# Weights laid out by the host in the units in which they are loaded

## The chip, the cores and the metric

The kernel runs on one core of one Trainium2 chip. The metric is the device time of one execution, in microseconds. Three runs of the kernel before took 2642.75, 2643.20 and 2644.79 us; the median is 2643.2 us.

## The reference

One sequence of 256 tokens with 1024 features passes through two blocks, each of two layers. All arrays are fp32. Cut to what carries the weights:

```python
# first block, l = 0, 1: a Fourier/convolution mixer (l = 0) or windowed attention (l = 1), then experts
shift, scale, gate = adaln(cond, ada_w[l, s], ada_b[l, s])       # ada_w[l, s]: [1024, 3072]
def ec_moe(h, router_w, router_b, w_gate, w_up, w_down):          # 16 experts, 32 tokens each
    ...
    xg = h[bidx, idx]
    hid = jax.nn.silu(jnp.einsum("becd,edf->becf", xg, w_gate)) * jnp.einsum("becd,edf->becf", xg, w_up)
    y = jnp.einsum("becf,efd->becd", hid, w_down) * gate[..., None].astype(h.dtype)
    return jnp.zeros_like(h).at[bidx, idx].add(y)

# second block, l = 0, 1: swiglu_ffn, three attentions side by side, swiglu_ffn
def swiglu_ffn(x, g, wi, wo):                                     # wi: [1024, 5632], wo: [2816, 1024]
    a, b = jnp.split(rms_norm_2(x, g) @ wi, 2, axis=-1)
    return (jax.nn.silu(a) * b) @ wo
```

Each expert's `w_gate`, `w_up` and `w_down` is a matrix of 1024 by 1024, which makes 12.6 MB for an expert and 201 MB for the experts of a layer. All other weights of both blocks together are some 290 MB, most of them in the second block.

## The kernel before

**Units of weight.** Every large weight reaches SBUF in units of 1 or 2 MB, each a tile `w` of 128 partitions. A unit is a block of rows and columns of the weight as it stands in HBM. Row k * 128 + p of the block goes to partition p, so what one partition receives is several rows, each contiguous in HBM for the width of the block alone: 512 columns (2 KB) for `ada_w`, `fc_w_in`, `attn_w_qkv` and most of the second block, 256 columns (1 KB) for the second block's output matrices, 1024 columns (4 KB) for the experts, `fc_w_out` and `attn_w_out`. `load_unit` (lines 209 to 212) issues the DMA on SP's queue. In `moe` (lines 798 to 808) a unit holds 256 rows of `w_gate` and the same 256 rows of `w_up` of one expert, and two DMAs of 1 MB fill it (line 801); the 16 matmuls of line 808 that use the unit read both parts at once, so they wait for both. A unit of `w_down` is one DMA of 2 MB (line 841), but for the last unit of the last expert, which comes in four DMAs of 0.5 MB. `attn_w_out` (lines 387 to 392) comes in four DMAs of 1 MB, each to 64 partitions, since the rows of two heads have to be interleaved.

**Buffers and queue.** In the first block a ring of seven 2 MB buffers (line 868) holds the units, and `moe` has two more of its own (`unit`, lines 789 to 794). SP issues the loads in one order for the whole program; a load is issued when its buffer has been read by the last matmul of the unit that held it before. So the loads run ahead of TensorE by up to nine units, and stop when all buffers are full. The second block has a ring of four buffers (line 1740).

**Order.** The instructions are recorded in program order and a scheduler sets the order on each engine, from its own estimate of when each operand is there. A load's estimated time is part of that.

**Other queues at the start.** `setup` (lines 244 to 267) issues the constants `cst` and `vec` on SP ahead of the first units, `x`, `positions` (256 integers to 128 partitions) and `msk` on ScalarE's queue, and small tables and `fou` on GpSimd's queue. `positions` starts the rotary tables (`rope_setup`, line 517 on), whose `Sin` on ScalarE (line 536) stands ahead of the first norm there. VectorE's line 531 and GpSimd's line 424 are two steps of that time that the prediction names.

**The names in the trace.** `wh` and `wl` are the two parts into which ScalarE (line 218) and VectorE (line 219) split a weight for all products but those of the experts and of adaLN. Line 278 is adaLN's product, line 808 the experts' first product, line 846 the second. Lines 1113 to 1115 are the three passes of a product of the second block. In the trace's names of DMA queues, q1 is SP's, q10 ScalarE's, q0 GpSimd's; q8 and q14 fetch the engines' instructions and tables, not data of the kernel.

Of the kernel before, what the change touches and what calls it, by code (L numbers as in the profile page):

```python
# [28 lines left out]
# columns of the fp32 constant block  # L29
# [15 lines left out]
# exp(-ln(10000) * i * 2 / d) in float32, as bit patterns  # L45
# [7 lines left out]
def host_constants2():  # L53
# [23 lines left out]
    # block n of group g: the first half of tokens 16 n.., the second half of tokens 16 (n + 1).., and the offsets  # L77
# [5 lines left out]
def host_constants():  # L83
# [12 lines left out]
    # Fourier matrices over the sequence (256) and over a group's features (128)  # L96
# [6 lines left out]
    # additive masks: identity and triangles, as bfloat16 words  # L103
# [5 lines left out]

class Halves:  # L110
    """Chunks 0-3 and 4-7 in two tiles."""
# [7 lines left out]
class Norm:  # L119
    """A norm whose row factors (rs, RS) may come after the products that they scale have begun."""  # L120


class Net:
# [32 lines left out]
    def rsqrt(self, out, ss, scale, eps, pool, tag, bufs=2):  # L156
        """out = (ss * scale + eps) ** -0.5 by Newton's iteration on VectorE."""
# [38 lines left out]
    def row_ss(self, pool):  # L196
        """Sums of squares of all rows: column t for token tile t."""
# [24 lines left out]
    def dense(self, xh, xl, wdram, n0, n, evac, cpool):  # L222
        """Token-layout product [256, n] of the split x^T and columns n0.. of a [1024, N] weight."""
# [4 lines left out]
    def dense_steps(self, xh, xl, wdram, n0, n, evac, cpool):  # L228
        nc = self.nc
        w = self.load_unit(wdram[:, n0:n0 + n].rearrange("(k p) n -> p k n", p=P), [P, KC, n])  # L230
# [50 lines left out]
    def ada_affine(self, l, s, g, router=False):  # L281
        """Per-feature factor and offset (as columns) of the modulated norm."""
# [18 lines left out]
        # the router takes the factor into its weights and the offset into its bias  # L301
# [15 lines left out]
    def ada_gate(self, l, s):  # L317
        """The gate row on all partitions; for the experts columns 256 j.. on partitions 32 j.."""
# [3 lines left out]
        for j0 in range(2):  # L322
            # the bias joins on the diagonal
# [18 lines left out]
    def normed(self, pool, dst):  # L342
        """dst = x / rms(x), token layout."""
# [11 lines left out]
    def transposed(self, xn, emit):  # L355
        """Transposes the 1024 features of both token tiles; emit(k, psum [128, 256])."""
# [10 lines left out]
    def mod_split(self, pool, xn, A, B, tag):  # L367
        """(xn * A + B)^T in split form."""
# [43 lines left out]
    def mixer(self, ada):  # L412
        nc, a = self.nc, self.a
        with ExitStack() as es:
# [20 lines left out]
            win = a["fc_w_in"][0]  # L435
# [5 lines left out]
            # depthwise convolution: four taps of 32 channels fill the contraction, four groups run side by side  # L441
# [1378 lines left out]
```

## Time and profile before

| | |
|---|---|
| time, median of three runs | 2643.2 us |
| span of the profiled execution, first to last instruction | 2640.8 us |
| TensorE matmul busy | 2193.6 us (83%) |
| HBM read | 695.28 MB, 264 GB/s over the span |
| packets on SP's queue | 270800, 693.52 MB, 71.7% of 16 DMA engines |
| issues of `moe_w_gate` and `moe_w_up` | 128 each, 1024 KB |
| issues of `moe_w_down` | 62 of 2048 KB, 8 of 512 KB |

The span is cut into stages by what runs: the mixer to about 190 us, the experts of layer 0 to about 642 us, windowed attention to about 803 us, the experts of layer 1 to about 1254 us, and from there the second block. A view by slices or by stretches gives for each the busy time of the engines, the TensorE clock that was granted, the busy share of the 16 DMA engines and the rate in GB/s. A view of the DMA packets in a window gives their number by queue, the bytes, and the time that the packets took as a share of 16 engines; a share above 100% means that packets overlap a little on an engine. Packets under 512 bytes are the 4-byte writes that end each transfer, but for a few small constants.

### The profile page before, as it was taken

Reading aid. Unit: us, or ns where it says so; the run is one execution under the profiler, and the core shown is the slowest. Engines: PE = TensorE matmul, PEld = TensorE weight load, DVE = VectorE, ACT = ScalarE, POOL = GpSimd, SP = SyncE. Lnnn points to the kernel's source line nnn. Section 1 sums busy time; section 2 is a strip of 40 time slices with the busy share of each in tenths; the row PEclk is TensorE's granted clock in tenths of the full one; section 3 lists DMA queues with packets and bytes.
Section 4 is the critical chain, followed back from the end, with each engine's and each line's share of the span. In section 5 each row is a group of like instructions: output and inputs, shape, how many; then the busy total and the mean of one; then the engine's idle time right before and its main releaser. Section 6 shows DMA issues by size and latency. Waiting matters only on the chain.

```text
span 2640.8 us, 39018 instructions
## 1 busy us (share of the span) xinstructions
PE 2193.6 (83%) x16264; PEld 1610.6 (61%) x16264; DVE 1175.8 (45%) x2258; ACT 885.5 (34%) x1494; POOL 92.4 (3%) x137
## 2 busy tenths in 40 slices
PE   5977655555987555555999999999999999999999
PEld 3542111112553111111899978799999997789997
DVE  4451101102662101010755567775565566677663
ACT  4430000002441000000544565554444446655443
POOL 1100000000000000000100010000000000000000
PEclk9988768888998888888999999999999999999999
DMA  9989999999968999999555553255555555324553
GB/s 361 333 341 409 409 409 409 409 409 401 307 247 356 409 409 409 409 409 408 192 185 181 162 173 99 78 178 177 180 187 189 174 178 181 109 84 138 182 186 118
DMA packets 272224, 698.86 MB, mean 265 GB/s; under 512 B 9792, under 2 KB 66896, under 8 KB 272048
## 3 DMA queue, kind: packets, MB, share of 16 engines
q1 hardware_dynamic: 270800, 693.52, 71.7%
q8 instruction: 128, 2.10, 0.3%
q0 software_dynamic: 544, 1.60, 0.3%
q10 hardware_dynamic: 704, 1.25, 0.1%
q14 instruction: 48, 0.39, 0.0%
HBM read 695.28 MB, written 1.05 MB: 264 GB/s over the span
## 4 chain that ended last, share of the span: by engine, by line
PE 48%; ACT 1%; DVE 1%; DMA 0%; issue 0%; POOL 0%; ACTq 0%; DVEq 0%
PE mm L1115 11%; PE mm L1114 11%; PE mm L1113 11%; PE at L1687 1%; PE at L1113 1%; PE at L1115 1%; PE at L1114 1%; PE mm L1070 1%; PE mm L1069 1%; PE mm L1071 1%; PE tr L1229 1%; PE oa L1699 1%; PE oa L1352 1%; ACT wh L218 1%; DVE wl L219 1%; PE at L1391 0%
## 5 line engine op out<-in xcount | busy, mean ns | idle before, releaser
L219 DVE TENSOR_TENSOR wl<-w,wh 128x1024 fp32r<-128x1024 f32 (+3 forms) x494 | 551.0, 1118 | 396.1 <-ACT wh L218 379.9
L218 ACT CAST wh<-w 128x1024 fp32r<-128x1024 f32 (+3 forms) x494 | 472.5, 959 | 590.0 <-PE mm L1114 415.8
L808 PE MATMUL mm<-w,xg 128*32 128x512 f32 x2048 | 326.4, 766 | 237.9 <-DMA w<-in_moe_w_up_dram 236.4
L1114 PE MATMUL mm<-hl,wh 128*128 128x256 f32 x1728 | 490.3, 284 | 2.5 <-DVE hl L958 2.5
L1115 PE MATMUL mm<-hh,wl 128*128 128x256 f32 x1728 | 490.6, 284 | 0.0
L1113 PE MATMUL mm<-hh,wh 128*128 128x256 f32 x1728 | 490.5, 284 | 0.0
L808 PEld LDWEIGHTS mm<-w,xg 128*32 128x32 f32 x2048 | 69.8, 128 | 459.5 <-issue 362.8
L1114 PEld LDWEIGHTS mm<-hl,wh 128*128 128x128 f32 x1728 | 326.1, 189 | 4.3 <-DVE hl L958 3.1
L1115 PEld LDWEIGHTS mm<-hh,wl 128*128 128x128 f32 x1728 | 326.1, 189 | 3.7 <-issue 3.4
L1113 PEld LDWEIGHTS mm<-hh,wh 128*128 128x128 f32 x1728 | 326.0, 189 | 0.6 <-issue 0.3
L828 ACT ACTIVATE sil<-mm 128x256 f32<-128x256 f32 x32 | 12.3, 384 | 802.9 <-PE mm L808 802.9
L846 PE MATMUL at<-w,hidT 128*32 128x256 f32 x2048 | 165.9, 481 | 93.5 <-DMA w<-in_moe_w_down_dram 84.0
L829 DVE TENSOR_TENSOR hid<-mm,sil 128x256 f32<-128x256 f32 x32 | 13.6, 425 | 506.5 <-ACT sil L828 506.5
L846 PEld LDWEIGHTS at<-w,hidT 128*32 128x32 f32 x2048 | 76.1, 135 | 174.6 <-DMA w<-in_moe_w_down_dram 81.5
L854 DVE TENSOR_TENSOR xh<-at,agm 32x256 f32<-32x256 f32 x128 | 53.8, 420 | 281.0 <-PE at L846 279.6
L1114 PE MATMUL mm<-gl,wh 128*128 128x256 f32 x528 | 149.3, 283 | 0.0
L1115 PE MATMUL mm<-gh,wl 128*128 128x256 f32 x528 | 148.8, 282 | 0.0
L1113 PE MATMUL mm<-gh,wh 128*128 128x256 f32 x528 | 148.5, 281 | 0.0
L1113 PEld LDWEIGHTS mm<-gh,wh 128*128 128x128 f32 x528 | 99.9, 189 | 0.0
L1115 PEld LDWEIGHTS mm<-gh,wl 128*128 128x128 f32 x528 | 99.5, 189 | 0.0
L1114 PEld LDWEIGHTS mm<-gl,wh 128*128 128x128 f32 x528 | 98.9, 187 | 0.0
L278 PE MATMUL oa<-w,condp 128*32 128x512 f32 x384 | 55.4, 637 | 7.0 <-DMA w<-in_ada_w_dram 6.2
(574 smaller groups left out, 3343.3 us busy)
## 6 DMA issues: line engine op xcount, KB each, us to landing
w<-in_moe_w_gate_dram SPq DMA_DIRECT2D x128, 1024.0 KB, 18.9
w<-in_moe_w_up_dram SPq DMA_DIRECT2D x128, 1024.0 KB, 18.6
w<-in_moe_w_down_dram SPq DMA_DIRECT2D x62, 2048.0 KB, 23.0
w<-in_ffn_wi_dram SPq DMA_DIRECT2D x88, 1024.0 KB, 5.2
w<-in_ada_w_dram SPq DMA_DIRECT2D x24, 2048.0 KB, 19.7
w<-in_w_in_dram SPq DMA_DIRECT2D x40, 1024.0 KB, 5.1
w<-in_ffn_wo_dram SPq DMA_DIRECT2D x35, 1024.0 KB, 5.1
w<-in_ffn_wo_dram SPq DMA_DIRECT2D x12, 768.0 KB, 4.9
```

The lines of the kernel that those rows point to most:

```text
L218: self.nc.scalar.copy(wh, w)
L219: self.nc.vector.tensor_sub(wl, w, wh.bitcast(F32))
L278: nc.tensor.matmul(ps[32 * j:32 * j + 32, :], self.condp[:, k, 3 - row:35 - row], w[:, k, :], start=first and r == 0, stop=last and r == 1)
L808: nc.tensor.matmul(ps[32 * j:32 * j + 32], xg[:, k, e * CAP:(e + 1) * CAP], w[:, :, kk, j * 256:(j + 1) * 256], start=k == 0, stop=k == KC ...
L846: nc.tensor.matmul(psd[32 * j:32 * j + 32, :], hT2[:, k % 2, 32 * (k // 2):32 * (k // 2) + 32], w[:, kk, j * 256:(j + 1) * 256], start=k = ...
L854: nc.vector.tensor_tensor(dst, psd[32 * j:32 * j + 32, :], gate[32 * j:32 * j + 32, :], op=ALU.mult)
L1069: nc.tensor.matmul(ps[t], xh[:, k, sl], wh[:, c, :], start=k == 0, stop=False)
L1070: nc.tensor.matmul(ps[t], xl[:, k, sl], wh[:, c, :], start=False, stop=False)
L1071: nc.tensor.matmul(ps[t], xh[:, k, sl], wl[:, c, :], start=False, stop=k == kc - 1)
L1113: nc.tensor.matmul(o, wh[:, cs], xh[:, k, :], start=k == 0 and j == 0, stop=False, skip_group_check=True)
L1114: nc.tensor.matmul(o, wh[:, cs], xl[:, k, :], start=False, stop=False, skip_group_check=True)
L1115: nc.tensor.matmul(o, wl[:, cs], xh[:, k, :], start=False, stop=k == kc - 1 and j == 1, skip_group_check=True)
```

## The change

The host packs each large weight into the units in which the kernel loads them, a partition's part of a unit contiguous. `pack` writes one array for a weight and layer: unit after unit, and in each unit partition after partition. `UNITS` lists the blocks, in the order and of the sizes in which the kernel asks for them, and `Packed.unit` finds one. A load is then a DMA of 128 rows, each as long as a partition's whole part: 16 KB for the 2 MB units of the first block, 8 KB for a 1 MB unit of the second. The bytes in SBUF are where they were. The gate and up rows of an expert's unit lie beside each other in `moe_w_gate_up` and come in one DMA of 2 MB. `attn_w_out` is packed with its heads already in the order in which the two halves were filled, and comes in two DMAs of 2 MB to 128 partitions. The last unit of `w_down` of the last expert still comes in four DMAs, each with 4 KB for a partition. Small tables, `x` and the constants are loaded as before. The diff also takes out comments and the unused `load8`; lines move by that, nothing else. Its core:

```diff
+def _blocks(kc, m, n0, n):
+    return [(k, min(m, kc - k), n0, n) for k in range(0, kc, m)]
+UNITS = {
+    "ada_w": lambda l: [(0, KC, 512 * j, 512) for j in range(6)],
+    "fc_w_in": lambda l: [(0, KC, 512 * j, 512) for j in range(3)],
+    "attn_w_out": lambda l: _blocks(KC, 4, 0, D),
+    "ffn1_wi_2": _ff_in,
...
+class Packed:
+    def __init__(self, ap, name, l):
+        self.ap, self.at, off = ap, {}, 0
+        for k0, m, n0, n in UNITS[name](l):
+            self.at[k0, n0] = (off, m, n)
+            off += P * m * n
+    def unit(self, k0, m, n0, n):
+        off, m_, n_ = self.at[k0, n0]
+        assert (m, n) == (m_, n_), (k0, m, n0, n)
+        return self.ap[off:off + P * m * n].rearrange("(p x) -> p x", p=P)
+def pack(w, name, l):
+    out = []
+    for k0, m, n0, n in UNITS[name](l):
+        out.append(w[P * k0:P * (k0 + m), n0:n0 + n].reshape(m, P, n).transpose(1, 0, 2).ravel())
+    return np.concatenate(out)
...
-    def load_unit(self, src, shape, eng=None):
+    def W(self, name, *i):
+        return Packed(self.a["_".join(map(str, (name, *i)))], name, i[-1])
+    def load_unit(self, src, shape):
         w = self.T(self.ring, shape, "w", self.wbufs)
-        (eng or self.nc.sync).dma_start(w, src)
+        self.nc.sync.dma_start(w if len(shape) == 2 else w.rearrange("p k n -> p (k n)"), src)
...
-        w = self.load_unit(self.a["ada_w"][l, s, :, j0 * 512:(j0 + 1) * 512].rearrange("(k p) n -> p k n", p=P),
-                           [P, KC, 512])
+        w = self.load_unit(self.W("ada_w", l, s).unit(0, KC, j0 * 512, 512), [P, KC, 512])
...
-            n = P // len(wdram[u])
-            for i, src in enumerate(wdram[u]):
-                nc.sync.dma_start(w[n * i:n * i + n], src)
+            nc.sync.dma_start(w.rearrange("p k n -> p (k n)"), wdram.unit(4 * u, 4, 0, D))
...
-                    for i, nme in enumerate(("moe_w_gate", "moe_w_up")):
-                        nc.sync.dma_start(w[:, i], a[nme][l, e, u * 256:(u + 1) * 256, :]
-                                          .rearrange("(k p) f -> p k f", p=P))
+                    nc.sync.dma_start(w.rearrange("p g k f -> p (g k f)"), a["moe_w_gate_up"][l, e, u])
...
-                        r0 = u * 512 + c * P
-                        nc.sync.dma_start(w[:, c:c + step], a["moe_w_down"][l, e, r0:r0 + step * P, :]
-                                          .rearrange("(k p) f -> p k f", p=P))
+                        nc.sync.dma_start(w[:, c:c + step].rearrange("p k f -> p (k f)"),
+                                          a["moe_w_down"][l, e, u, :, c * D:(c + step) * D])
...
-            w = self.load_unit(wsrc[h * P:(h + m) * P, n0:n0 + n].rearrange("(k p) n -> p k n", p=P), [P, m, n])
+            w = self.load_unit(wsrc.unit(h, m, n0, n), [P, m, n])
...
+    gu = np.stack([f("moe_w_gate"), f("moe_w_up")], axis=2).reshape(2, NE, 2, 4, 2, P, D)
+    d["moe_w_gate_up"] = np.ascontiguousarray(gu.transpose(0, 1, 3, 5, 2, 4, 6)).reshape(2, NE, 4, P, 4 * D)
+    dn = f("moe_w_down").reshape(2, NE, 2, 4, P, D)
+    d["moe_w_down"] = np.ascontiguousarray(dn.transpose(0, 1, 2, 4, 3, 5)).reshape(2, NE, 2, P, 4 * D)
```

**SP's queue, first expert of layer 0.** `w` is the unit, `128x2x1024` and `128x4x1024` are its shape in SBUF as the DMA writes it. Before, the last two of the four gate and up pairs and the expert's two units of `w_down`:

```order
L801 DMA w_1358<-in_moe_w_gate_dram 128x2x1024
L801 DMA w_1358<-in_moe_w_up_dram 128x2x1024
L801 DMA w_1380<-in_moe_w_gate_dram 128x2x1024
L801 DMA w_1380<-in_moe_w_up_dram 128x2x1024
L841 DMA w_1472<-in_moe_w_down_dram 128x4x1024
L841 DMA w_1490<-in_moe_w_down_dram 128x4x1024
```

After, the same units, and the first of the next expert:

```order
L865 DMA w_1356<-in_moe_w_gate_up_dram 128x4096
L865 DMA w_1377<-in_moe_w_gate_up_dram 128x4096
L903 DMA w_1468<-in_moe_w_down_dram 128x4096
L903 DMA w_1486<-in_moe_w_down_dram 128x4096
L865 DMA w_1510<-in_moe_w_gate_up_dram 128x4096
```

Each pair has become one DMA, and every DMA writes 4096 elements in one run for a partition. SP's whole list has 574 rows before and 446 after; the difference is the 128 pairs, and nothing in it has changed places.

**TensorE, windowed attention of layer 1, between the two layers of experts.** `oa` is the accumulator of adaLN's product (line 278 before, 348 after), `tr` a transpose of softmax weights, `mm<-spT` weighted values. Before, from the start of the adaLN product:

```order
L278 MATMUL oa_3887<-w_3888,condp_98 32x512 x8
L278 MATMUL oa_3887<-w_3898,condp_98 32x512 x5
L638 MATMUL tr_3583<-cst_72,se_3566 128x128 x4
L638 MATMUL tr_3592<-cst_72,se_3567 128x128 x4
L278 MATMUL oa_3887<-w_3898,condp_98 32x512 x3
L278 MATMUL oa_3887<-w_3908,condp_98 32x512
L649 MATMUL mm_3599<-spT_3588,v_3074 64x256
L649 MATMUL mm_3599<-spT_3597,v_3074 64x256
L649 MATMUL mm_3599<-spT_3588,v_3074 64x256
L649 MATMUL mm_3599<-spT_3597,v_3074 64x256
L278 MATMUL oa_3887<-w_3908,condp_98 32x512 x7
L278 MATMUL oa_3887<-w_3918,condp_98 32x512 x5
```

After, from the start of the same product:

```order
L348 MATMUL oa_3823<-w_3824,condp_98 32x512 x8
L348 MATMUL oa_3823<-w_3834,condp_98 32x512 x8
L348 MATMUL oa_3823<-w_3844,condp_98 32x512 x5
L705 MATMUL tr_3519<-cst_72,se_3502 128x128 x4
L705 MATMUL tr_3528<-cst_72,se_3503 128x128 x4
L348 MATMUL oa_3823<-w_3844,condp_98 32x512 x3
L348 MATMUL oa_3823<-w_3854,condp_98 32x512
L716 MATMUL mm_3535<-spT_3524,v_3010 64x256
L716 MATMUL mm_3535<-spT_3533,v_3010 64x256
L716 MATMUL mm_3535<-spT_3524,v_3010 64x256
L716 MATMUL mm_3535<-spT_3533,v_3010 64x256
L348 MATMUL oa_3823<-w_3854,condp_98 32x512 x7
```

The scheduler now takes adaLN's second chunk whole ahead of the transposes, where it took 5 of its 8 matmuls, and the third and fourth come sooner by as much. Such moves stand between the two layers of experts on TensorE, VectorE and ScalarE; in the mixer, the experts and the second block the order on the engines is as before.

## Rows read from the trace of the kernel before

**Rows 1.** The profile page: span, busy time, and busy tenths in 40 slices.

```profile
span 2640.8 us, 39018 instructions
...
PE 2193.6 (83%) x16264; PEld 1610.6 (61%) x16264; DVE 1175.8 (45%) x2258; ACT 885.5 (34%) x1494; POOL 92.4 (3%) x137
...
DMA  9989999999968999999555553255555555324553
GB/s 361 333 341 409 409 409 409 409 409 401 307 247 356 409 409 409 409 409 408 192 185 181 162 173 99 78 178 177 180 187 189 174 178 181 109 84 138 182 186 118
```

**Rows 2.** Busy time by stretch: start, end, length, engines, PEclk, DMA share, GB/s.

```profile
0.00:190.00 190.00, 146.91 (x938) 87.70 (x939) 93.42 (x195) 76.49 (x148) 23.59 (x24) 0.93 0.93 345
190.00:215.00 25.00, 24.54 (x232) 12.44 (x234) 8.30 (x16) 5.99 (x10) 0.00 (x0) 1.00 0.99 389
215.00:642.00 427.00, 249.60 (x1926) 74.98 (x1914) 38.21 (x83) 12.63 (x31) 0.00 (x0) 0.79 1.03 409
642.00:803.00 161.00, 139.14 (x748) 86.36 (x741) 104.61 (x270) 72.97 (x180) 8.08 (x5) 0.93 0.82 278
803.00:830.00 27.00, 26.05 (x240) 12.77 (x238) 8.73 (x17) 6.38 (x11) 0.00 (x0) 0.99 1.01 401
830.00:1254.00 424.00, 238.92 (x1902) 73.59 (x1900) 37.79 (x82) 10.96 (x29) 0.81 (x2) 0.84 1.03 409
1254.00:2641.00 1387.00, 1368.40 (x10304) 1262.80 (x10300) 884.72 (x1595) 700.09 (x1085) 59.88 (x106) 1.00 0.49 159
```

**Rows 3.** Waits, 190 to 645 us: us in total, times, longest us.

```profile
PE mm L808 <- DMA w<-in_moe_w_up_dram: 117.0, 49, 3.3
...
PE at L846 <- DMA w<-in_moe_w_down_dram: 37.8, 19, 3.0
```

**Rows 4.** DMA packets by queue, 40 to 80 us (share of 16 engines).

```profile
DMA packets 7632, 15.44 MB, mean 386 GB/s; under 512 B 112, under 2 KB 112, under 8 KB 7628
...
q1 hardware_dynamic: 7628, 15.39, 103.9%
```

**Rows 5.** DMA packets by queue, 215 to 625 us.

```profile
DMA packets 43031, 167.69 MB, mean 409 GB/s; under 512 B 2137, under 2 KB 2137, under 8 KB 43015
...
q1 hardware_dynamic: 43015, 167.44, 102.3%
```

**Rows 6.** DMA packets by queue, 1283.2 to 1284 us: one packet alone.

```profile
q14 instruction: 1, 0.01, 2.4%
```

**Rows 7.** DMA packets by queue, 360.6 to 362.2 us.

```profile
q8 instruction: 1, 0.02, 4.2%
```

**Rows 8.** DMA packets by queue, 19 to 21 us.

```profile
q0 software_dynamic: 112, 0.57, 72.3%
q1 hardware_dynamic: 115, 0.24, 30.9%
```

**Rows 9.** Start of the program: one issue (KB, landing us), then timeline rows.

```profile
posi<-in_positions_dram ACTq DMA_DIRECT2D x1, 1.0 KB, 11.1
...
12.90 0.17 DVE L517 CAST posf<-posi 128x2 f32<-128x2 int32 x1 [2.37 <-DMA posi<-in_positions_dram]
...
15.10 6.38 DVE L531 TENSOR_SCALAR ang<-ang 128x64 f32<-128x64 f32 x1
...
22.00 0.26 ACT L536 ACTIVATE cos<-angn 128x64 f32<-128x64 f32 x1 [9.87 <-DVE angn L533]
...
14.22 0.50 POOL L264 CAST mskb<-mskf 128x384 bf16<-128x384 f32 x1 [10.37 <-DMA mskf<-in_msk_dram]
...
17.65 3.77 POOL L424 TENSOR_TENSOR wd<-cst,V 128x1024 f32<-128x1024 f32 x2
```

**Rows 10.** Timeline of PE in the attention of the first block.

```profile
712.84 3.62 PE L278 MATMUL oa<-w,condp 128*32 128x512 f32 x26
```

**Rows 11.** Chain that ended last, 2175 to 2225 us: start us, us, what.

```profile
2180.09 5.47 DMA w<-in_w_in_dram
...
2218.71 5.33 DMA w<-in_w_in_dram
```

More of the change, by code (lines that the diff above doesn't have):

```diff
@@ L107, in host_constants, with _ff_in, _ff_out, _w_in @@
     return {"cst": c, "fou": fou, "msk": msk}
+def _blocks(kc, m, n0, n):
+    return [(k, min(m, kc - k), n0, n) for k in range(0, kc, m)]
+def _ff_in(_):
+    out = []
+    for f0 in range(0, FF, 512):
+        n = min(512, FF - f0)
+        for c in (f0, FF + f0):
+            out += _blocks(KC, 2048 // n, c, n)
+    return out
+def _ff_out(l, last):
+    return _blocks(FF // P, 2, 0, D) if last and l else sum((_blocks(FF // P, 8, 256 * m, 256) for m in range(4)), [])
+def _w_in(_):
+    cols = [(0, 512), (512, 512), (1024, 512), (1536, 416), (1952, 512), (2464, 384), (2848, 408)]
+    cols += [(3256 + 512 * i, 512) for i in range(6)]
+    return sum((_blocks(KC, 4, n0, n) for n0, n in cols), [])
+UNITS = {
+    "ada_w": lambda l: [(0, KC, 512 * j, 512) for j in range(6)],
+    "fc_w_in": lambda l: [(0, KC, 512 * j, 512) for j in range(3)],
+    "attn_w_qkv": lambda l: [(0, KC, 512 * j, 512) for j in range(3)],
+    "fc_w_out": lambda l: _blocks(KC, 4, 0, D),
+    "attn_w_out": lambda l: _blocks(KC, 4, 0, D),
+    "ffn1_wi_2": _ff_in,
+    "ffn2_wi_2": _ff_in,
+    "ffn1_wo_2": lambda l: _ff_out(l, False),
+    "ffn2_wo_2": lambda l: _ff_out(l, True),
+    "w_in_2": _w_in,
+    "proj_sb_2": lambda l: [(0, 4, 512 * h, 512) for h in range(2)],
+    "proj_mla_2": lambda l: [(0, 4, 512 * h, 512) for h in range(2)],
+    "proj_nsa_2": lambda l: [(0, 4, 512 * h, 512) for h in range(2)],
+    "w_out_2": lambda l: [(0, KC, 256 * m, 256) for m in range(4)],
+    "mla_w_uq_2": lambda l: [(0, 2, 0, 768)],
+    "cmp_wk1_2": lambda l: [(0, 16, 0, P)],
+    "cmp_wv1_2": lambda l: [(0, 16, 0, P)],
+}
+class Packed:
[9 more added lines that the diff above has]
+def pack(w, name, l):
+    out = []
+    for k0, m, n0, n in UNITS[name](l):
+        out.append(w[P * k0:P * (k0 + m), n0:n0 + n].reshape(m, P, n).transpose(1, 0, 2).ravel())
+    return np.concatenate(out)
 class Halves:
@@ L119 @@
 class Norm:
+    pass
 class Net:
@@ L229, in dense_steps @@
         nc = self.nc
-        w = self.load_unit(wdram[:, n0:n0 + n].rearrange("(k p) n -> p k n", p=P), [P, KC, n])
+        w = self.load_unit(wdram.unit(0, KC, n0, n), [P, KC, n])
         ps = [self.mm([P, n]) for _ in range(2)]
@@ L506, in mixer @@
             gate = ada.gate
-            self.out_residual([(yh, yl, k) for k in range(KC)],
-                              [[a["fc_w_out"][0][512 * u:512 * (u + 1), :].rearrange("(k p) n -> p k n", p=P)]
-                               for u in range(2)], gate, p, lambda: ada('P4'), ("xn", 1))
+            self.out_residual([(yh, yl, k) for k in range(KC)], self.W("fc_w_out", 0), gate, p, lambda: ada('P4'),
+                              ("xn", 1))
     def rope_setup(self):
@@ L674, in windowed @@
             ada()
-            wout = a["attn_w_out"][0]
-            self.out_residual([(oh[k // 4], ol[k // 4], k % 4) for k in range(KC)],
-                              [[wout[512 * u + 256 * g:512 * u + 256 * g + 256, :].rearrange("(r d) n -> d r n", d=64)
-                                for g in range(2)] for u in range(2)], gate, p, None, ("se", 3))
+            self.out_residual([(oh[k // 4], ol[k // 4], k % 4) for k in range(KC)], self.W("attn_w_out", 0), gate, p,
+                              None, ("se", 3))
     def moe(self, l, A, B, rwA, rb, gate_fn):
@@ L1081, in gemmT @@
             m = min(2048 // n, kc - h)
-            w = self.load_unit(wsrc[h * P:(h + m) * P, n0:n0 + n].rearrange("(k p) n -> p k n", p=P), [P, m, n])
+            w = self.load_unit(wsrc.unit(h, m, n0, n), [P, m, n])
             for q in range(0, m, 1024 // n):
@@ L1152, in ffn @@
                 for k in range(0, nk, 2):
-                    w = self.load_unit(wo[k * P:(k + 2) * P, :].rearrange("(k p) n -> p k n", p=P), [P, 2, D])
+                    w = self.load_unit(wo.unit(k, 2, 0, D), [P, 2, D])
                     parts += [self.split(self.hp, w[:, c, :], [P, D]) for c in range(2)]
@@ L1434, in prep_ml @@
                     nc.scalar.activation(cT[:, c, :], ps, AF.Copy, scale=g)
[L1435 removed]
+                wuq = self.load_unit(self.W("mla_w_uq_2", l).unit(0, 2, 0, 768), [P, 2, 768])
                 wukv = self.load_unit(a["mla_w_ukv_2"][l], [P, D])
@@ L1556, in compress @@
                 for kind in range(2):
-                    w1 = self.load_unit(a["cmp_wv1_2" if kind else "cmp_wk1_2"][l].rearrange("(k p) n -> p k n", p=P),
-                                        [P, 16, P])
+                    w1 = self.load_unit(self.W("cmp_wv1_2" if kind else "cmp_wk1_2", l).unit(0, 16, 0, P), [P, 16, P])
                     w2 = self.T(p, [P, 64], "cw2", 2)
```

38 lines of the change are left out of this document (22 added, 16 removed).

## Prediction

> **What bounds the kernel now.** Read the page first. The span is 2640.8 us [rows 1]. Its line of 40 slices of DMA share stands at 9 for nearly all of the first half and at 5 or less after it, and the GB/s line is flat at 409 for most of that first half. So there are two kernels in one: a first block that may be bound by its loads, and a second that isn't. The view by stretches says which stage is which [rows 2]. From 215 to 642 and from 830 to 1254 us, the experts, TensorE is busy for 249.60 of 427 and 238.92 of 424 us, while the DMA share is 1.03 at 409 GB/s. From 1254 us on TensorE is busy for 1368.40 of 1387 us and the DMA share is 0.49. The mixer (0 to 190 us) and the attention (642 to 803 us) lie between: TensorE is busy for 146.91 of 190 and 139.14 of 161 us. Then the waits, to see who waits in the experts: TensorE waits 117.0 us for the up rows and 37.8 us for `w_down` in one layer [rows 3]. So the experts' end is set by the rate at which DMA brings 201 MB a layer, and only a change of that rate, or of the bytes, moves it. The other stages are bound by work on the engines, which the change leaves alone.
>
> What sets the rate is read from the packets. From 40 to 80 us the loads are all of 2 KB runs: 7628 packets on SP's queue, 112 of them under 512 bytes, at 386 GB/s [rows 4]. That is 7516 packets of 2 KB in 40 us on 16 engines, 16 * 40 / 7516 = 85.2 ns for one. From 215 to 625 us the runs are of 4 KB: 43015 - 2137 = 40878 packets in 410 us, 160.5 ns each, at 409 GB/s [rows 5]. Twice the bytes take 75.3 ns more, so 85.2 - 75.3 = 9.9 ns of a packet don't depend on its length.
>
> **The packet of 16 KB.** The change makes each run of a 2 MB unit 16 KB long. The straight line through the two points gives 9.9 + 8 * 75.3 = 612 ns, against 4 * 160.5 = 642 ns for the same bytes now: 4.6% less, 428 GB/s. No packet of that length stands on SP's queue in this trace, so the price is bounded by other rows. Below: without any fixed part it is 8 * 75.3 = 602 ns, 6.2% less. Nearest on the line: one 8 KB packet, alone on its queue, took 2.4% of 16 engines in 0.8 us, 0.31 us [rows 6]; the line gives 311 ns, so it holds to twice the length measured, with one engine at work. With all engines at work, 112 packets of 5 KB and 115 packets of 2 KB went in 2 us [rows 8], 16 * 2 / 113.5 = 282 ns for a pair; the line gives 198 + 85 = 283. Above: the one kind of 16 KB packet that the trace has, an instruction fetch, took 4.2% of 16 engines in 1.6 us, 1.08 us [rows 7]. I take 612, since rows 6 and 8 lie on its line, and the packet of rows 7 is not data on its way to SBUF tiles.
>
> A rule of the Trainium skill speaks against any gain: "DMA: Bandwidth & Descriptors", section Specifications, gives 512 B as the smallest transfer for line rate, so that 2, 4 and 16 KB would run alike and the sum would be nothing. Rows 4 and 5 do not agree with it: 386 against 409 GB/s, both with the engines full.
>
> **The sum for the experts.** The DMA share is full from the first unit after each stage's start: 0.99 from 190 to 215 us and 1.01 from 803 to 830 us [rows 2]. So the stretches that go with the packet's price are 190 to 642 and 803 to 1254 us, 452 + 451 = 903 us. Each ends with four 0.5 MB pieces whose runs stay 4 KB; at 409 GB/s they take 5.1 us a layer, so 893 us are left. 4.6% of it is **41 us**. If only the stretches counted in which TensorE is seen to wait (427 + 424 - 10 = 841 us), it would be 39; at 602 ns, 55. TensorE doesn't take over as the bound: 249.60 us of work stand in a stretch that would still last 407.
>
> One DMA in place of two for gate and up: the matmuls of a unit read both parts and wait for both already, so nothing waits longer. 128 issues fewer on SP cost nothing and save nothing while the DMA engines are full. The engines stay full as long as issues run ahead, which the nine buffers give: I cost that at nothing. If that cover were gone, a unit's load would show as a gap in the DMA share.
>
> **The mixer.** Its end is set by engine work; the loads run ahead. But one thing moves at the start. Rows 8 show that two queues share an engine packet by packet, 112 to 115. `positions` stands on ScalarE's queue beside the first units: 256 integers of 4 bytes, 16 on each engine, 11.1 us from issue to landing [rows 9]. Each may now wait behind 612 ns in place of 85: at most 16 * 0.53 = 8.4 us later. It releases line 517 on VectorE at 12.90 us, which would come to 21.3. From there line 531 stands 2.2 us on and took 6.38 us, until GpSimd's line 424 (from 17.65 us) was through; but GpSimd waits at line 264 for `msk`, which stands behind `positions` on the same queue, so its steps go back as well and line 531 runs free. The `Sin` at 22.00 us, for which ScalarE waits 9.87 us, then comes at about 24, 2 us late, and the first norm behind it. If `positions` is not late and `msk` is, it comes up to 2 us early. I take **+1 us**, ends -2 and +2.
>
> **The attention.** `attn_w_out` comes with 128 partitions in place of 64, which frees DMA time in a stage whose DMA share is 0.82 [rows 2]; TensorE doesn't wait for a load there. The scheduler's moves put adaLN's chunks, 26 of their matmuls seen at 712.84 us in a row of 3.62 us [rows 10], up to one head sooner. Their data, issued before, are there earlier than now. I cost this at 0; the bound is that row's length either way, 3.6 us.
>
> **The second block.** The runs go from 1 and 2 KB to 8 KB, and TensorE is the bound. Twice on the chain a load of 1 MB stands, 5.47 and 5.33 us [rows 11]: 32 packets of 85.2 ns become 8 of 311 on each engine, 2.73 to 2.49 us. That is 0.24 us each, **-0.5 us** together; from 0 to -2.
>
> Sum: -41 + 1 - 0.5 = -40.5 us, from a span of 2640.8 to 2600.3. The median of the runs, 2643.2, stands 2.4 us above the profiled span; with the same difference the time is **2603 us**.
>
> **The rivals.**
>
> *No gain in the experts.* The 16 KB run is cut into 4 KB packets, or something that all engines share caps them at 409 GB/s. For it: no packet above 4 KB stands on SP's queue, and 409 is the highest rate that lasts anywhere in the trace. Against it: rows 6 and 8 show packets of 8 and 5 KB on other queues, and rows 8 add up to the line's time with all engines at work. What is left is +1 - 0.5: 2644 us.
>
> *A smaller fixed part.* If the 2 KB stretch was slowed by something besides its packets, the line is too steep at its foot. With 3.5 ns of 160.5 fixed, 16 KB take 642 - 3 * 3.5 = 631.5 ns, 1.6% less: 14.6 us, 2629 us. The same page of the Trainium skill, section "Why small descriptors are slow", has about 3 cycles for each packet, 3.5 ns at the 850 MHz that it gives; by it the sum would be this one. Rows 4 and 5, 9.9 ns, do not agree.
>
> *The long packet is slow.* The 16 KB packets run like the instruction fetch of rows 7, at 1.08 us. The experts' loads then take 893 * (1.08 / 0.642 - 1) = 609 us more, 3252 us. It decides from 642 ns on: each 10 ns above that cost 893 * 10 / 642 = 14 us, so at 650 ns the time is already 2655. For it: it is the only 16 KB packet here. Against it: the 8 KB packet of rows 6, also not the kernel's own data, lies on the line.
>
> **How the numbers follow.** The forecast, 2588 to 2622 us, has a chance of 0.62: the line holds for the packets of 5 and 8 KB that the trace shows. No gain, 2640 to 2647, has 0.17; the smaller fixed part, around 2629, 0.07; the long packet slow, from 2648 up, 0.10; a gain beyond the slope alone, below 2588, 0.04. The range reaches from 2588 (all of the fixed part gone) through the case of no gain, to 2647; it leaves out 0.04 and 0.10. About 0.2%, 5.3 us, is what a measurement of this kernel can tell from no change: 2637.9 to 2648.5 is the same. Faster: 0.62 + 0.07 + 0.04 = 0.73; same 0.17; slower 0.10. The likeliest case's own range is 2588 to 2622.
>
> **What the profile after would show.** In the experts, packets of 16 KB on SP's queue, about 1.6 a us and engine, at about 428 GB/s with the share still full; the first layer's experts end near 623 us, the second's near 1214, and the second block takes 1387 us as now. If the packets are 4 KB and the rate 409, the run is cut; if the packets are long and the rate is 409, all engines share a cap; if the share falls below full in the experts, the issues no longer run ahead. At the start, line 517 later than 12.90 us shows `positions` behind the long packets, and `Sin` after 24 us would make the mixer's term too small. A wait of TensorE for a load in the mixer or the attention, or a changed length of the second block beyond 2 us, would make the prediction wrong.

## The result and the profile after

The changed kernel takes 2611.4 us (median of four runs, 2605.4 to 2612.0) against 2643.9 us for the kernel before on the same chip: a ratio of 0.9873, 95% interval [0.9859, 0.9887]. The profiled execution spans 2609.5 us, 31.3 less than before. The forecast was 2603 us, 40.5 less; the time is in the forecast's own range, 8.4 us above the forecast.

First the stages. The edges are TensorE's first product of a layer of experts and the end of the last one. The rows of the kernel after, from TensorE's timeline (start, us, what; in brackets the wait before it):

```profile
188.22 3.34 PE L871 MATMUL mm<-w,xg 128*32 128x512 f32 x16 [0.71 <-ACT xg L848]
...
625.24 1.08 PE L908 MATMUL at<-w,hidT 128*32 128x256 f32 x8 [1.82 <-DMA w<-in_moe_w_down_dram]
...
785.54 3.35 PE L871 MATMUL mm<-w,xg 128*32 128x512 f32 x16 [0.71 <-ACT xg L848]
...
1223.43 0.64 PE L908 MATMUL at<-w,hidT 128*32 128x256 f32 x8 [1.82 <-DMA w<-in_moe_w_down_dram]
```

The same four edges of before stand at 186.15, 642.29, 798.05 and 1255.42 us. That gives, in us (the last stage ends with the span):

| stage | before | after | change | forecast |
|---|---|---|---|---|
| mixer, to the first product of the experts | 186.2 | 188.2 | +2.1 | +1 (-2 to +2) |
| experts, layer 0 | 456.1 | 438.1 | -18.0 | -41 for both (-39 to -55) |
| attention | 155.8 | 159.2 | +3.5 | 0 (-3.6 to +3.6) |
| experts, layer 1 | 457.4 | 438.5 | -18.8 | |
| second block | 1385.4 | 1385.4 | 0 | -0.5 (-2 to 0) |

Busy time by stretch, after (start, end, length; TensorE, weight loads, VectorE, ScalarE, GpSimd; granted clock, DMA share, GB/s):

```profile
215.00:626.00 411.00, 247.13 (x1942) 72.94 (x1934) 38.19 (x83) 12.63 (x31) 0.00 (x0) 0.81 1.01 427
626.00:788.00 162.00, 138.73 (x734) 86.12 (x734) 104.83 (x270) 72.63 (x180) 7.76 (x5) 0.90 0.69 274
788.00:815.00 27.00, 27.00 (x250) 13.13 (x242) 8.30 (x16) 6.00 (x10) 0.00 (x0) 0.99 0.93 385
815.00:1224.00 409.00, 248.62 (x1913) 73.20 (x1910) 38.20 (x83) 11.35 (x30) 0.81 (x2) 0.79 1.01 426
1224.00:2610.00 1386.00, 1369.18 (x10296) 1263.26 (x10292) 884.49 (x1595) 700.06 (x1085) 59.84 (x106) 1.00 0.45 158
```

The experts are still bound by their loads: the share is as full as in [rows 2], TensorE's work is the same 248 us, and only the rate has moved, from 409 to 427 GB/s. The packets in the first layer's experts say why (number by queue, MB, share of 16 engines):

```profile
DMA packets 11277, 164.30 MB, mean 427 GB/s; under 512 B 1248, under 2 KB 1248, under 8 KB 1248
...
q1 hardware_dynamic: 11260, 164.04, 100.3%
```

The window is 215 to 600 us. 11260 - 1248 = 10012 packets of 16 KB in 385 us on 16 engines are 615.3 ns for one, where [rows 5] had 4 * 160.5 = 642 ns for the same bytes. That is 4.16% less, and 4.16% of the 893 us that the forecast counted is 37.1 us; 36.8 were measured. The waits of TensorE there shrank with it, from the 117.0 us of [rows 3] to 105.2:

```profile
PE mm L871 <- DMA w<-in_moe_w_gate_up_dram: 105.2, 48, 3.3
...
PE at L908 <- DMA w<-in_moe_w_down_dram: 37.2, 22, 2.7
```

So of the 9.2 us between the forecast's 40.5 and the 31.3 of this span, 4 lie in the size of the main term, 1 in the mixer, 3.5 in the attention and 0.5 in the second block.

### The profile page after: what moved, and what is told of

Read it like the earlier page. It is cut to its first block, busy times and chain, and to the rows that moved or that the text cites. A ratio compares the mean times of both kernels' runs of the same rounds, so it can differ in the third digit from the quotient of the medians.

```text
span 2609.5 us, 38749 instructions
## 1 busy us (share of the span) xinstructions
PE 2200.1 (84%) x16264; PEld 1608.1 (62%) x16264; DVE 1173.0 (45%) x2258; ACT 885.2 (34%) x1494; POOL 92.3 (4%) x137
## 4 chain that ended last, share of the span: by engine, by line
PE 50%; ACT 1%; DVE 1%; issue 0%; POOL 0%; ACTq 0%; DVEq 0%
PE mm L1174 11%; PE mm L1173 11%; PE mm L1172 11%; PE mm L1129 1%; PE mm L1128 1%; PE mm L1130 1%; PE at L1745 1%; PE at L1172 1%; PE at L1173 1%; PE at L1174 1%; PE tr L1288 1%; PE oa L1757 1%; PE oa L1411 1%; ACT wh L289 1%; PE at L1450 0%; PE at L1437 0%
## 5 line engine op out<-in xcount | busy, mean ns | idle before, releaser
L871 PEld LDWEIGHTS mm<-w,xg 128*32 128x32 f32 x2048 | 64.1, 125 | 439.1 <-DMA w<-in_moe_w_gate_up_dram 321.7
L348 PE MATMUL oa<-w,condp 128*32 128x512 f32 x384 | 54.8, 636 | 11.9 <-DVE condp L939 11.1
```

The costliest lines, as they stand in the source:

```text
L348: nc.tensor.matmul(ps[32 * j:32 * j + 32, :], self.condp[:, k, 3 - row:35 - row], w[:, k, :], start=first and r == 0, stop=last and r == 1)
L871: nc.tensor.matmul(ps[32 * j:32 * j + 32], xg[:, k, e * CAP:(e + 1) * CAP], w[:, :, kk, j * 256:(j + 1) * 256], start=k == 0, stop=k == KC ...
```

## Which part of the change pays: the experts' weights alone, and all the others

The first two runs split the change. One packs the experts' weights alone:

```diff
 kernel before, and in moe:
-                    for i, nme in enumerate(("moe_w_gate", "moe_w_up")):
-                        nc.sync.dma_start(w[:, i], a[nme][l, e, u * 256:(u + 1) * 256, :]
+                    nc.sync.dma_start(w.rearrange("p g k f -> p (g k f)"), a["moe_w_gate_up"][l, e, u])
 (w_down likewise, and its two arrays on the host)
```

> Kernel before, with only w_gate, w_up and w_down packed (16 KB runs, gate and up in one DMA). The order on all engines is that of before. Theory: the gain is the packet's price in the experts (614 ns against 642, 18.0 + 18.8 us), and what it lost against the forecast came from the other weights' layout: 2.1 us at the start (positions behind long packets) and 3.5 us in the attention (another order of instructions). So here the experts start at 186 us and last 438 us each, the attention lasts 156 us, the second block 1385 us: 2607 us, 4 to 5 below the changed kernel. Rival: the attention's 3.5 us come from what the shorter experts leave behind (buffers, granted clock), not from the order: then it lasts 159 us here too and the time is 2610.

The other packs everything but them, so that `moe` and its arrays are those of before and the rest is that of after.

> Changed kernel, with w_gate, w_up and w_down as before (4 KB runs, two DMAs for gate and up). The order on the engines is that of the changed kernel. Theory: nothing is gained; the start costs 2.1 us and the attention 3.5 us, the second block nothing: 2649 us against 2643.9. Rival (the other weights' layout costs nothing by itself): 2644; if their long runs help the mixer or the second block: below 2643.

The experts alone took 2606.3 us (2604.1 to 2607.7), ratio 0.9859 [0.9846, 0.9873]. In the profile the experts start at 185.6 us and last 438.2 and 439.0 us, the attention 156.9: as the theory had it. The rest alone took 2644.7 us, ratio 1.0007 [0.9999, 1.0016]: nothing gained, and nothing lost that can be told from zero. Its mixer ended at 188.1 us, late as in the changed kernel, but its attention lasted 156.1 us, with the changed kernel's order of instructions. The theory had 159 for it, and 2649 us. So the whole gain is in the experts, the mixer's 2 us come with the other weights, and the order is in doubt as the cause of the attention's 3.5 us.

## The packet's price, length by length

The forecast took the price of a 16 KB packet from a straight line through 2 and 4 KB. Two runs put other lengths into the experts, with the units, their buffers and their order as in the changed kernel (one run each, 2657.5 and 2631.4 us; they are read by their profiles):

```diff
-    d["moe_w_gate_up"] = ... .reshape(2, NE, 4, P, 4 * D)
+    RUNS = (2, 8)     # runs for a partition in layer 0, 1; the other kernel: (2, 4)
+            v = v.reshape(*v.shape[:2], P, RUNS[l], 4 * D // RUNS[l]).transpose(0, 1, 3, 2, 4)
...
+            self.nc.sync.dma_start(w.rearrange("p (r x) -> p r x", r=R), src.rearrange("r p x -> p r x"))
 in the other kernel, layer 0 alone:
+            for r in range(R):
+                self.nc.sync.dma_start(w[:, r * (4 * D // R):(r + 1) * (4 * D // R)], src[r])
```

> Changed kernel with other run lengths in the experts, one DMA for a unit as there: 8 KB in layer 0, 2 KB in layer 1. Theory (a part of each packet that doesn't depend on its length): 8 KB packets take 308 to 311 ns, so layer 0 lasts 439 to 443 us against 438.1; 2 KB packets take 85 ns as at the start of the program, 682 ns for 16 KB, so layer 1 lasts 457.4 * 682 / 642 = 486 us. Rival (smaller fixed part, 3.5 ns, the 2 KB stretch at the start slowed by something else): layer 1 lasts about 467 us. Rival (from 2 KB on all lengths run alike, what helped was the one DMA): layer 1 lasts 438.

> Changed kernel with other DMAs in the experts: in layer 0 each unit comes in two DMAs with 8 KB for a partition, in layer 1 in one DMA with 4 KB runs. Theory (the length of the packet alone): layer 0 lasts as with 8 KB runs in one DMA, 439 to 443 us; layer 1 as before the change, 457 us. Rival (fewer DMAs, or an expert's gate and up rows beside each other, bring the gain): layer 1 lasts 438 to 445 us, layer 0 more than 450.

Packets in the first kernel's layer 0 (8 KB runs, one DMA, 215 to 600 us) and layer 1 (2 KB runs, 830 to 1230 us):

```profile
DMA packets 20966, 161.82 MB, mean 420 GB/s; under 512 B 1227, under 2 KB 1227, under 8 KB 1227
...
q1 hardware_dynamic: 20949, 161.57, 101.0%
```

```profile
DMA packets 76599, 154.64 MB, mean 387 GB/s; under 512 B 1184, under 2 KB 1184, under 8 KB 76585
...
q1 hardware_dynamic: 76585, 154.43, 104.2%
```

And in the second kernel's layer 0 (8 KB runs, two DMAs, 215 to 600 us) and layer 1 (4 KB runs, one DMA, 830 to 1200 us):

```profile
DMA packets 22185, 161.68 MB, mean 420 GB/s; under 512 B 2464, under 2 KB 2464, under 8 KB 2464
...
q1 hardware_dynamic: 22169, 161.43, 101.0%
```

```profile
DMA packets 38066, 151.34 MB, mean 409 GB/s; under 512 B 1158, under 2 KB 1158, under 8 KB 38052
...
q1 hardware_dynamic: 38052, 151.12, 102.2%
```

Taken as above (packets of SP's queue less those under 512 bytes, 16 engines):

| run | packets, us | one packet | 16 KB | GB/s | experts of the layer |
|---|---|---|---|---|---|
| 2 KB | 75401 in 400 | 84.9 ns | 679 ns | 387 | 483.5 us |
| 4 KB, one DMA | 36894 in 370 | 160.5 ns | 642 ns | 409 | 457.4 us |
| 8 KB, two DMAs | 19705 in 385 | 312.6 ns | 625 ns | 420 | 445.1 us |
| 8 KB, one DMA | 19722 in 385 | 312.3 ns | 625 ns | 420 | 444.1 us |
| 16 KB (changed kernel) | 10012 in 385 | 615.3 ns | 615 ns | 427 | 438.1 us |

Each doubling adds 75.6, 151.8 (2 * 75.9) and 303.0 ns (4 * 75.75): a straight line of 75.8 ns for 2 KB and 9 ns for the packet itself, over the whole range. Both rivals for this are out. With 3.5 ns fixed, 2 KB would have given 467 us and not 483.5; and 4 KB runs in one DMA from one contiguous 2 MB gave exactly the time of before, 457.4, so neither the merged DMA nor the nearness of gate and up rows in HBM earns anything. How far apart a partition's runs lie in HBM doesn't show either: with 8 KB in one DMA its two runs stand 1 MB apart, with two DMAs each DMA reads 1 MB in one piece, and a packet took 312.3 and 312.6 ns. The table also disagrees with the Trainium skill, "DMA: Bandwidth & Descriptors", section Specifications, which gives 512 B as the smallest transfer for line rate: from 2 to 16 KB the rate still rises by 10%.

## The mixer: short transfers behind long packets

At the start the trace shows what the forecast described, and one thing that it did not. Line 423 (353 before) is VectorE's half of the first norm, line 361 (291) ScalarE's copy of adaLN's product, which TensorE makes in line 348 (278). Timeline before, of the rows that [rows 9] doesn't have:

```profile
25.87 0.88 DVE L353 TENSOR_SCALAR xn<-x,rstd 128x512 f32<-128x512 f32 x2
...
28.54 7.13 PE L278 MATMUL oa<-w,condp 128*32 128x512 f32 x48
...
35.75 0.59 ACT L291 COPY arow<-oa 128x512 f32<-128x512 f32 x1 [8.54 <-PE oa L278]
```

Timeline after:

```profile
19.54 0.17 DVE L584 CAST posf<-posi 128x2 f32<-128x2 int32 x1 [8.93 <-DMA posi<-in_positions_dram]
...
21.39 0.19 DVE L598 TENSOR_SCALAR ang<-ang 128x64 f32<-128x64 f32 x1
...
22.11 0.26 ACT L603 ACTIVATE cos<-angn 128x64 f32<-128x64 f32 x1 [9.89 <-DVE angn L600]
...
24.97 0.50 POOL L335 CAST mskb<-mskf 128x384 bf16<-128x384 f32 x1 [21.13 <-DMA mskf<-in_msk_dram]
...
25.98 4.72 DVE L423 TENSOR_SCALAR xn<-x,rstd 128x512 f32<-128x512 f32 x2
...
28.40 4.06 POOL L492 TENSOR_TENSOR wd<-cst,V 128x1024 f32<-128x1024 f32 x2
...
30.39 7.18 PE L348 MATMUL oa<-w,condp 128*32 128x512 f32 x48
...
37.65 0.59 ACT L361 COPY arow<-oa 128x512 f32<-128x512 f32 x1 [10.34 <-PE oa L348]
```

`positions` lands 17.8 us after its issue, where [rows 9] had 11.1, and line 584 (517 before) runs 6.6 us later. Line 598 (531 before) runs free in 0.19 us, and `Sin` comes at 22.11, where [rows 9] had 22.00. But GpSimd's `wd` has moved from 17.65 to 28.40 us with the late `msk`, and VectorE's step that takes long beside it is now line 423: 4.72 us for its two instructions, 0.88 before. TensorE's transposes wait for it, and line 348's row starts 1.85 us later. In this profile line 361 runs at 37.65 where before it ran at 35.75, and these 1.9 us are still there when the experts start. In the third profile of the same kernel (two more runs of it follow below) line 423 is as late, but line 361 runs earlier:

```profile
36.41 0.58 ACT L361 COPY arow<-oa 128x512 f32<-128x512 f32 x1 [9.13 <-PE oa L348]
```

There line 348's row took 5.99 us in place of 7.18; from 30 to 34 us the granted clock was 0.79 in the third profile and 0.50 in the first. So the lateness of line 423 is worth 1.85 us at line 348, and TensorE's clock there decides how much of that arrives.

Why `positions` is late shows in the packets from 13 to 15 us after: SP's units and ScalarE's queue, one for one.

```profile
q1 hardware_dynamic: 63, 0.84, 98.6%
q10 hardware_dynamic: 63, 0.02, 4.3%
```

Of SP's 63, 51 are packets of 16 KB (0.84 MB), the others 4-byte writes that end a unit; of ScalarE's, 14 are rows of `msk`, which follow `positions`. From 9 to 12 us, with `positions` alone on ScalarE's queue, the trace has 59 packets of 16 KB and 56 of 4 bytes. So each 4-byte packet of `positions`, sixteen on an engine, waits for about one packet of 16 KB, 0.62 us. The Trainium skill, "DMA: Bandwidth & Descriptors", section "Queues, rings and completion order", says that an engine drains some 9 to 17 descriptors of one queue before it turns to the next; counted in the packets of the trace that does not hold here, since then all sixteen would have passed in one or two turns.

The test is to issue the short ones first. One run puts `positions` and `msk` ahead of `x`, all on ScalarE's queue:

```diff
-            for t in range(2):
-                nc.scalar.dma_start(self.x[:, t, :], a["x"][0, t * P:(t + 1) * P, :])
             self.pos = self.T(self.ap, [P, 2], "posi", 1, I32)
             nc.scalar.dma_start(self.pos, ...)
             nc.scalar.dma_start(mskf, a["msk"])
+            for t in range(2):
+                nc.scalar.dma_start(self.x[:, t, :], a["x"][0, t * P:(t + 1) * P, :])
```

> Changed kernel, but positions and msk are issued on ScalarE's queue ahead of x. Theory: the start waits for positions (line 584 ran at 19.54 us) since each of its 4-byte packets waits behind 16 KB packets; issued first it meets none, line 584 runs by 10 us, the first norm is through by 16 us instead of 26, and the experts start 5 to 10 us sooner, at 178 to 183 us: 2601 to 2606. Rival (the first units of ada_w bound the start, and positions only fills their time): the fourth unit is there at about 26 us, the experts start at 186 to 188 and the time is 2609 to 2611.

It took 2608.5 us (2602.8 to 2612.5); the experts start at 188.3 us. The theory's number fell, and not for the rival's reason. ScalarE's timeline of this run (line 271 squares `x` for the first norm):

```profile
15.36 0.60 ACT L271 ACTIVATE mm<-x 128x512 f32<-128x512 f32 x1 [11.29 <-DMA x<-in_x_dram]
...
22.98 0.60 ACT L271 ACTIVATE mm<-x 128x512 f32<-128x512 f32 x1 [3.79 <-DMA x<-in_x_dram]
```

Line 584 did run at 3.94 us. But now `x`, 4 KB packets issued 1 us later than before, went one for one with the 16 KB packets, and the norm had to wait for it until 23 us. What had been cured in one transfer came back in the next: the norm's factor stood at 26.45 us, 25.79 in the changed kernel. VectorE's line 598, now beside GpSimd's steps again, took 6.39 us, and line 423, clear of them, 0.88. Line 361 ran at 36.19, 0.2 us before that of the third profile; from 169 to 172 us this run fell 1 us behind it, where its granted clock was 0.50 and the third's 1.00. So the following run puts `x` on SP's queue ahead of the first unit, and lets GpSimd's steps wait for the first norm, so that they don't run beside it:

```diff
+            for t in range(2):
+                nc.sync.dma_start(self.x[:, t, :], a["x"][0, t * P:(t + 1) * P, :])
...
 (fou, the memsets of x4 and wd now stand behind self.normed(p, xn))
+            nc.vector.tensor_copy(fou[:, 0:2], xn[:, 1, 510:512])
+                nc.vector.tensor_copy(x4s[G][:, 0, 0:2], xn[:, 1, 510:512])
+                    nc.vector.tensor_copy(wds[G][:, 0, 0:2], xn[:, 1, 510:512])
```

> Changed kernel, but all that the start waits for is issued ahead of the first 16 KB packets: positions and msk on ScalarE's queue, then x on SP's queue between vec and the first unit; GpSimd's fou, its two memsets and its two first steps of wd wait for the first norm. Theory (short transfers wait behind long packets; with positions first alone it was x that came late, its last part at 22.98 us): the norm's factor is there at 13 to 15 us instead of 25.8, line 361's copy is set by the fourth unit of ada_w and runs at 28 to 31 us instead of 37.65, the experts start at 179 to 183 us instead of 188.2: 2602 to 2606. Rival (TensorE and the loads take the time back later in the mixer): the experts start at 186 or later, 2609 or more.

2604.5 us (2603.2 to 2605.9), against 2607.3 for the changed kernel in the same comparison. The norm's factor is there at 15.36 us instead of 25.79, near what was expected, and line 423, with GpSimd's steps behind it, took 0.89 us. But line 361 runs at 33.91 and the experts start at 185.0, 2 to 3 us sooner than in the three profiles of the changed kernel and not 5 to 9. TensorE's timeline says what is late next, the units themselves:

```profile
26.83 3.37 PE L348 MATMUL oa<-w,condp 128*32 128x512 f32 x16 [3.97 <-DMA w<-in_ada_w_dram]
31.92 1.92 PE L348 MATMUL oa<-w,condp 128*32 128x512 f32 x16 [1.72 <-DMA w<-in_ada_w_dram]
```

If the loads bound the start now, then what shares the engines with the first four units must cost. The last step moves `bro`, `router_w` and `fou` behind adaLN's factor, by a small copy from it into each as above, on top of the run before:

> The kernel with the short loads first, and with bro, the two router_w and fou issued only once adaLN's factor is there, so that they don't share the engines with ada_w's four units; line nsink goes to the attention. Theory (the loads now bound the start: there the third and fourth unit were waited for 3.97 and 1.72 us, the fourth until 31.92): the 0.8 MB that move and bro's sixteen packets of 1.4 us, one on each engine, give 1.5 to 3.5 us, the fourth unit is there at 28.5 to 30.5, the experts start at 182 to 184 instead of 185.0: 2601 to 2603.5. Rival (something later than the loads sets the mixer's end): no change, 2604.5; or fou, now late, is waited for in the mixer: more than 2605.

2602.5 us (2599.4 to 2606.0), against 2608.5 for the changed kernel beside it; ratio to before 0.9845 [0.9831, 0.986]. The fourth unit is there at 28.27 us and not at 31.92, 3.65 us sooner, so the loads did bound that point (`bro`'s sixteen packets had taken 1.06 us each in the mean, not 1.4):

```profile
28.27 3.10 PE L348 MATMUL oa<-w,condp 128*32 128x512 f32 x16 [2.99 <-DMA w<-in_ada_w_dram]
```

The experts start at 183.3, only 1.7 us sooner. A part of the gain went at once: these sixteen products took 3.10 us in place of 1.92, with a granted clock of 0.61 (28.2 to 31.4 us) in place of 1.00. This median is the lowest of the kernels here. That it is faster than the changed kernel beside it, at 0.9872 [0.9856, 0.9889], is likely but not shown: the intervals just overlap, and so do those of the run before it, 0.9848 [0.9834, 0.9863], and the changed kernel beside that, 0.9865 [0.9848, 0.9881]. In the profiled execution the attention was long (158.4 us, next section).

## The attention: the order or the clock

The changed kernel's 3.5 us in the attention had two candidates: the scheduler's new order and the granted clock. The order of before comes back if `attn_w_out` alone is loaded in four DMAs of 64 partitions (16 KB runs stay):

```diff
-            nc.sync.dma_start(w.rearrange("p k n -> p (k n)"), wdram.unit(4 * u, 4, 0, D))
+            src = wdram.unit(4 * u, 4, 0, D)
+            step = 64 if not tag[0] == "xn" else P
+            for p0 in range(0, P, step):
+                nc.sync.dma_start(w[p0:p0 + step].rearrange("p k n -> p (k n)"), src[p0:p0 + step])
```

> Changed kernel, but attn_w_out comes in four DMAs of 64 partitions each, still in 16 KB runs. That alone gives the order of before on TensorE, VectorE and ScalarE in the attention. Theory (the order is what costs 3.5 us in the attention): it lasts 156 us instead of 159.2, the time is 2608. Rival (the granted clock, which fell in another place): 159 us, 2611.

It took 2607.8 us (2606.1 to 2608.9) with an attention of 155.7 us: what the theory of the order had forecast. Taken alone it would have settled the matter in its favour. The run with the rest packed, 156.1 us in the changed order, spoke against it, so the changed kernel was run again, twice, with nothing altered.

> The changed kernel once more, for a second profile of the same instructions. So far the attention lasted 159.2 and 159.3 us where the changed kernel's order met packed experts, 156.1 with the same order and experts as before, 155.7 and 156.9 with the order of before. Where it was long, the granted clock was down in the first 8 us (0.68 and 0.59, else 0.97 to 1.00) and at 80 to 96 us of it (0.83 to 0.95, else 1.00). Theory (the clock): the attention is 155.5 to 157 us where these falls are missing in this profile, and 159 where they are there. Rival (the order): 159 us also with the clock at 1.00.

> The changed kernel a third time, for one more profile and more runs beside the other kernel on the same chip. Theory (the attention's length goes by where the granted clock falls, 155.3 or 159.2 us with the same instructions): this profile has one of the two lengths, with the clock to match, and the runs fall about 2606 or about 2611.5. Rival (a drift of the chip between comparisons): all runs of this comparison stand together in one place, with before moved by as much.

The medians were 2607.3 (2606.1 to 2612.2) and 2608.5 us (2603.7 to 2612.2), and in both profiles the attention lasted 155.3 us, with the same instructions in the same order as the 159.2. The third profile's edges:

```profile
624.03 0.64 PE L908 MATMUL at<-w,hidT 128*32 128x256 f32 x8 [0.22 <-DMA w<-in_moe_w_down_dram]
...
779.97 3.21 PE L871 MATMUL mm<-w,xg 128*32 128x512 f32 x16 [0.71 <-ACT xg L848]
```

So the order does not cost the 3.5 us. What differs is in the first product of the stage, line 922, the experts' last sums. TensorE's timeline, in the first profile and in the third:

```profile
627.29 5.75 PE L922 MATMUL at<-xh,oh 128*128 128x512 f32 x8 [0.97 <-DVE xh L916]
```

```profile
625.64 3.93 PE L922 MATMUL at<-xh,oh 128*128 128x512 f32 x8 [0.97 <-DVE xh L916]
```

The first 4 us of the attention and 4 us some 92 us into it, in the first profile (the last three columns are granted clock, DMA share, GB/s):

```profile
626.30:630.30 4.00, 3.03 (x8) 1.32 (x5) 2.38 (x5) 0.17 (x1) 0.00 (x0) 0.50 1.01 430
...
718.30:722.30 4.00, 4.00 (x20) 2.88 (x19) 2.30 (x11) 2.62 (x12) 0.00 (x0) 0.74 0.83 352
```

and in the third:

```profile
624.70:628.70 4.00, 3.06 (x7) 1.15 (x8) 3.07 (x6) 0.94 (x3) 0.00 (x0) 1.00 1.01 430
...
716.70:720.70 4.00, 4.00 (x27) 2.15 (x30) 3.29 (x12) 2.53 (x11) 0.00 (x0) 1.00 0.49 209
```

At 0.50, which is 1.2 in place of 2.4 GHz, line 922's eight products took 1.8 us longer. Counted from the stage's start, the first profile is 1.8 us behind the third at the first transpose of the norm, 1.3 at the products behind it, 2.9 at the first product with `attn_w_out` (after the second fall, at 92 us), and 3.9 at the stage's end. The last 1.0 us comes where the clock fell in both: 142 us after the stage's start in the first profile, 144 us after it in the third. The link with line 922 holds for all twelve profiles: where line 922's median product took 0.88 to 1.06 us (the changed kernel's first profile, `positions` first, and the tables late) the attention lasted 158.4 to 159.3 us; where it took 0.61 us, in the other nine, 155.3 to 156.9. The twelve runs of the changed kernel fall into two groups with nothing between, six at 2603.7 to 2608.0 and six at 2611.2 to 2612.2 us; the profiles of 155.3 us belong to the first, that of 159.2 to the second. The other nine runs have no profile, so that the attention parts them is likely but not shown. What sets the clock there stays open. TensorE had waited for the last piece of `w_down` before it, 1.82 us in the long one and 0.93 and 0.22 in the two short ones of the changed kernel; but with the experts packed alone it had waited 1.17 and kept its clock, and with the tables late 0.84 and lost it.

## Why the prediction was right, and where it was off

*The experts, -41: right in mechanism, off by a tenth in size.* The term that was mis-sized is the slope. The price of the 2 KB packet, 85.2 ns, was read from 40 us at the start of the program [rows 4]; over 400 us of experts the same packet takes 84.9 ns. The slope is carried on over seven steps of 2 KB: 75.3 ns for each and 9.9 fixed, where 75.8 and 9.0 are right, gave 612 ns for 16 KB in place of 615.3, 4.2 us of the 893. From 84.9 and 160.5 the same line gives 84.9 + 7 * 75.6 = 614.1 ns, so the 2 KB price is 1.8 ns of the miss; the 1.2 left are as much as 0.2 ns in the 4 KB price, seven times over. That the line could be carried to four times the longest length that SP's queue had shown was the real risk, and it held; the break-even of 642 ns was never near.

*The merged DMA, nothing.* Right: two DMAs or one for a unit, 312.6 and 312.3 ns a packet. The issues did run ahead: the share stayed full.

*The experts' ends.* Near 623 and 1214 us were named; they came at 626.3 and 1224.1 in the first profile, 624.7 and 1218.4 in the third, later by the mixer, the attention and the packet.

*The mixer, +1 (-2 to +2).* It was 2.1, 1.4 and 0.8 us in three profiles of the changed kernel (188.2, 187.5 and 187.0 us against 186.2). Line 584 late, line 598 free and `msk` late were as forecast; that `Sin` would come at 24 was too much by 2 us, since `positions` came at 19.5 and not at its bound of 21.3. The step that failed is that GpSimd's steps, once late, were let go: the forecast asked what their lateness frees (line 531) and not what they run into next (line 423, 1.9 us at TensorE's transposes). The three sizes differ by the granted clock in line 348's row: 7.18, 6.39 and 5.99 us. So the size near +1 is luck: the 2 us that the forecast gave to `Sin` did not come, and others that it had not seen came in their place.

*The attention, 0 (up to 3.6 either way).* Right for the change: 155.3 us in two of three profiles. The 3.5 us of the first profile lie inside the bound, but the bound's reason, a row of adaLN's products sooner or later, isn't what filled it; the clock did, which the forecast had not reckoned with here at all.

*The second block, -0.5.* 1385.4, 1383.8 and 1383.6 us in three profiles against 1385.4: between 0 and -1.8, as bounded. With the experts packed alone, where this block is that of before, it took 1386.3, so a term of 0.5 us can't be told from the spread of single profiles.

*The rivals.* No gain, a smaller fixed part and the slow long packet are all out by the table of lengths: 427 GB/s, 84.9 ns and 615.3 ns.

With these sizes the sum is -37 + 1.4 - 1 = -37 us for an execution whose clock holds, 2606 to 2607, and 3 to 4 us less gain for one whose clock falls at line 922. The medians of the two groups of runs, 2605.8 and 2612.1, stand 6 us apart; the 2 us beyond the attention were not taken apart.

## What to carry to other kernels

Where the loads set the pace and the DMA share is full, price the packet, not the DMA: measure two run lengths over long stretches, draw the line, and a longer run earns the fixed part (here 9 ns) for each packet saved, while merging DMAs or moving rows nearer to each other earned nothing here. Long packets had a price elsewhere: each packet of another queue waited for about one of them, so whatever the program waits for early has to be issued ahead of the first long one, all of it, or the wait moves to the next short transfer. An engine's step that comes late is to be followed to what it stands beside next. Before a few us between two profiles are put down to an order of instructions, look at the granted clock in the same stretch and profile the same kernel again.

## What had not been expected

That a 1 KB transfer can be set back by 6.7 us by the loads of another queue, without one byte more on it, and that putting it first sets back a 1 MB transfer in its place (the last part of `x` from under 11 to 23 us). And that the same instructions in the same order take 155.3 or 159.2 us for one stage, with the granted clock of TensorE at 0.50 or 1.00 over its first eight products.
